# Dilated attention in a two-layer decoder: values in 512-byte pieces, attended tiles two and two, softmax steps behind the scores

## The chip, the cores and the metric

One core of one Trainium2 chip runs the whole program. The metric is the device time of one execution in microseconds, the median over several; a profiled execution also has a span, from the first to the last instruction on record, which is a little shorter. TensorE is PE below (PEld its weight loads), VectorE is DVE, ScalarE is ACT, GpSimd is POOL, SyncE is SP.

## What is computed

A trunk of two layers on a sequence of 1024 tokens of width 1024, all float32: a gated short convolution, a dilated attention, and a SwiGLU feed-forward block (width 2816) behind each. The change lies in the attention, cut here to what matters:

```python
BRANCHES = ((128, 1), (512, 4), (2048, 16))          # window, dilation; 16 heads of 64

def dilated_branch(q, k, v, rel_bias, window, dilation):
    ...                                              # regroup the tokens by residue mod dilation
    s = einsum(qb, kk) * HEAD_DIM ** -0.5            # a block of queries on its own and the previous keys
    s = s + bias                                     # T5 relative bias of the head
    s = where(mask, s, NEG_INF)
    lse = logsumexp(s)
    return einsum(exp(s - lse), vv), lse

def dilated_attention_mixer(h, w_qkv, w_out, rel_bias):
    ...
    alpha = softmax(stack(lses))                     # mixes the branches
    o = sum(alpha * outs)
    return o @ w_out
```

## The kernel before

Products of float32 quality are made of three passes with operands split into a high and a low part. `split` (L145, L146) does it: ACT copies `w_hi` (rounded), DVE subtracts to get `w_lo`. Both engines execute in the order in which the program was written; so does PE, and so do the queues that issue DMAs (SP's for loads).

The attention goes over 16 heads in slots, `slot(n, ...)` for n = 0 to 16. Slot n computes the scores of head n and, beside them, the softmax and the product with the values (PV) of head n - 1; in between stand pieces of other matrix work, drawn one by one from `dense` by `other(k)`: value tiles of later groups (`v` evictions on ACT), the projections of queries and keys, and the output product, whose weights and whose attended tiles (`oin`) are split on ACT and DVE as they come.

- Scores (`scores`): seven steps s0 to s6. PE fills a bank, DVE adds the bias on the way out: lf in s0 and s1 (two adds each, L1585), lh in s2 (L1594, with a first maximum, L1599), ld and lp together in s3 to s6 (L1611, L1616; two maxima in s4, L1620 and L1622). Behind s6 stand two more maxima, and POOL reduces m over the partitions to mb (L1628), the maximum by which the head is normalised.
- Softmax (`softmax`): five steps, for lf, lh, ld, and the two halves of lp (384 and 512 columns). Each subtracts mb on DVE (L1636) and takes the exponential on ACT (L1637). Slots 0 to 13 do the steps of the previous head one by one, between their own score steps. For heads 13 to 15 they all run at the end of the head's own slot.
- PV (`values`, L1647): PE multiplies exponentials with `vx`, in the order lf, lh, then ld and lp in turns. The tile `vx` holds the values of a pair of heads and between them columns of ones, so that one matmul gives the output o and the sum z. ACT copies z (logarithm, L1670) and o (L1671) out.
- A pair's o is scaled (`finish`, `attended`) and written to DRAM (`odram`), and read back as `oin` for the output product.
- SP loads, at the start of slot n, the keys, the values of the pair that is next (`load_values`, in even heads), the queries and the bias of head n + 1.

The start of each step in a slot up to 13:

```python
                for i in range(8):
                    next(due[0], None)      # a softmax step of head n - 1
                    next(sc, None)          # a score step of head n
                    k = 1 + (i in EXTRA and n < LAG) if n else i % 2
                    other(k)                # k pieces of the other matrix work
```

Of the kernel before, what the change touches and what calls it, by code (L numbers as in the profile page):

```python
# [10 lines left out]
F32 = mybir.dt.float32  # L11
F32R = mybir.dt.float32r
AF = mybir.ActivationFunctionType
# [7 lines left out]
H = 16  # L21
# [28 lines left out]
AO = 4  # L50
LAG = 13
EXTRA = (3, 7)
FILL = (("v", 0), ("v", 1), ("v", 2), ("v", 3), ("qk", 7))
DENSE = (13,) * 13 + (16, 13, 12, 11)
DEEP_ORDER = (1, 2, 5, 6, 7, 3, 4)

# [40 lines left out]
def view(t, off, dims):  # L97
    return bass.AP(tensor=t.tensor, offset=t.offset + off, ap=[t.ap[0]] + [list(d) for d in dims])
# [3 lines left out]
def trunk(ctx: ExitStack, tc: tile.TileContext, x, gains_in, cwi, ck, cwo, wqkv, wo, relb,  # L102
          wg, wu, wd, oneh, ident, out):
    nc = tc.nc
# [9 lines left out]
    scope = {}  # L114
# [20 lines left out]
    def split(src, dst=None, eng=nc.vector):  # L135

        w = src.shape[1]
        if dst is None:
            if w <= HALF:
                t = page("w", F32R)  # L140
                dst = t[:, :w], t[:, HALF:HALF + w]
            else:
                dst = page("w_hi", F32R)[:, :w], page("w_lo", F32R)[:, :w]
        hi, lo = dst
        nc.scalar.activation(hi, src, AF.Copy)  # L145
        eng.tensor_tensor(out=lo, in0=src, in1=hi, op=ALU.subtract)  # L146
        return hi, lo
# [200 lines left out]
    add_units(QK, QK_PAIRS, lambda u, n: wqkv[(KT, 0)[n] + u])  # L348
    for kind, g in FILL:
        if kind == "v":  # L350
# [1114 lines left out]
    def load_bias(h):  # L1465
        t = scope["pool"].tile([128, L1 + L2], F32, name="bias", tag="bias", bufs=2)
        base = tables.offset + h * G3
        nc.sync.dma_start(t[:, 0:L1], bass.AP(tensor=tables.tensor, offset=base, ap=[[1, 8], [A1, 16], [1, L1]]))
        nc.sync.dma_start(t[:, L1:L1 + L2], bass.AP(tensor=tables.tensor, offset=base + G0,
                                                    ap=[[1, 32], [A2, 4], [1, L2]]))  # L1470
        return t
# [8 lines left out]
    def attention(norm, qk):  # L1480
# [2 lines left out]
        qlo = [scope["pool"].tile([128, S], F32R, name=f"ql{a}") for a in range(2)]  # L1483
        for a in range(2):
            nc.gpsimd.memset(qlo[a][64 - 64 * a:128 - 64 * a].bitcast(F32), 0.0)
        vx = scope["pool"].tile([128, 16, 192], F32, name="vx", tag="vx", bufs=1)
        nc.vector.memset(vx[:, :, 64:128], 1.0)

        def projections(p):

# [37 lines left out]

        def load_values(p):
            src = vdram[p // 2]  # L1530
            for a in range(2):
                off = src.offset + p % 2 * 128 + a * 64
                dims = slice(128 * a, 128 * a + 64)
                nc.sync.dma_start(vx[:, 0:8, dims], bass.AP(src.tensor, off, [[256, 128], [128 * 256, 8], [1, 64]]))
                for h in range(2):
                    nc.sync.dma_start(vx[:, 8 + 4 * h:12 + 4 * h, dims],
                                        bass.AP(src.tensor, off + 512 * 256 * h, [[1024, 128], [256, 4], [1, 64]]))

        def load_kq(n):

# [99 lines left out]
        def values(p, a, st):  # L1640
            lf, lh, ld, lp = (st[n] for n in ("lf", "lh", "ld", "lp"))
            acc = [bank(), bank()]
            kd = [[128, 4], [1, 32]]
            b1 = [[32, 16], [1, 8]]

            def mm(ih, off, dims, u, rhs, first=False, last=False):
                nc.tensor.matmul(view(acc[ih], off, dims), vx[:, u, 64 * a:64 * a + 128], rhs,  # L1647
                                 start=first, stop=last)

            for ih in range(2):  # L1650
                for r4 in range(4):
                    mm(ih, r4 * 32, kd, 8 + r4, view(lf, ih * HALF + r4 * 32, kd), first=r4 == 0)
                    if r4 % 2:
                        yield
            for r4 in range(4):
                mm(1, r4 * 32, kd, 12 + r4, view(lh, r4 * 32, kd))
                if r4 % 2:
                    yield
            for j in range(8):
                off = (j % 4) * 8  # L1660
                mm(j // 4, off, b1, j, view(ld, blk(j), b1), last=False)
                if j:
                    mm(j // 4, off, b1, j - 1, view(lp, blk(j), b1), last=j % 4 == 3)
                yield
            o, z = st["o"], st["z"]
            n0 = slice(64 * a, 64 * a + 64)
            z0 = slice(64 - 64 * a, 128 - 64 * a)
            for ih in range(2):
                s = slice(ih * HALF, (ih + 1) * HALF)
                nc.scalar.activation(z[n0, s], acc[ih][z0], AF.Ln)  # L1670
                nc.scalar.activation(o[n0, s], acc[ih][n0], AF.Copy)  # L1671
            yield

        def finish(p):
# [39 lines left out]
        put_off, ending, due = [], [], [iter(())]  # L1714
        OZ, acts = {}, {}

        def slot(n, dense, ndense, late=0, hook=iter(())):

            def other(k):
                for _ in range(k):  # L1720
                    next(dense, None)

            p, a = divmod(n, 2)
            if n < H:
                new = dict(bias=bias.pop(n))
                sc = scores(p, a, new)
            else:
                sc = iter(())
            if n + 1 < H:
                load_kq(n + 1)  # L1730
                bias[n + 1] = load_bias(n + 1)
            if n:
                q, b = divmod(n - 1, 2)
                if b == 0:
                    OZ[q] = page("o"), page("z")
                old = live.pop(n - 1)
                old.update(o=OZ[q][0], z=OZ[q][1])
                pv = values(q, b, old)
            else:
                pv = iter(())  # L1740
            extra = later = iter(())
            lagged = n <= LAG
            if n + 1 < H:
                later = classes(n + 1)
            if lagged and a and p:
                ending.append(finish(p - 1))
            used = 0
            if lagged:
                for i in range(8):
                    next(due[0], None)  # L1750
                    next(sc, None)
                    k = 1 + (i in EXTRA and n < LAG) if n else i % 2
                    other(k)
                    used += k
                    if a and ending and i == 4:
                        run(ending.pop())
                run(sc)
            else:
                if a == 0 and not late:
                    other(1)  # L1760
                    used += 1
                for i in range(8):
                    next(sc, None)
                    next(pv, None)
                    next(pv, None)
                    if i >= late and i % 2 == 0:
                        other(1)
                        used += 1
                run(sc)
                run(pv)  # L1770
                if a == 0:
                    extra = finish(p - 1)
                if a == 0 and n < H:
                    load_values(p)
            left = max(ndense - used, 0)
            for i in range(8):
                next(pv, None)
                next(pv, None)
                if i == (2 if n > LAG + 1 else 5):
                    attended()  # L1780
                if not lagged and (i < FIN0 or i > SOFT):
                    next(extra, None)
                if i in (1, 2):
                    next(later, None)
                if i < 4:
                    next(hook, None)
                if i == (3 if lagged else SOFT) and n < H:
                    live[n] = new
                    due[0] = softmax(new)
                    if n >= LAG:  # L1790
                        run(due[0])
                other(left * (i + 1) // 8 - left * i // 8)
            run(pv)
            run(extra)

        def load_attended(ps):
            raw = {p: page("oin") for p in ps}
            for p in ps:
                nc.sync.dma_start(raw[p], odram[p])
            return raw  # L1800
# [27 lines left out]
        done, first = {}, {}  # L1828
# [7 lines left out]
                        yield from value_tiles(g, j)  # L1836
            yield from out_product(0, range(AO), first)

        def halves():
            for q, t in done.items():  # L1840
                first[q] = split(t)
                yield

        dense = fill()
        for n in range(H):
            if n == LAG - 2:
                done.update(load_attended(range(AO)))
            hook = halves() if n == LAG - 2 else iter(())
            slot(n, dense, DENSE[n], 3 if n == H - 2 else 0, hook)
            run(hook)  # L1850
        acts.update(split_attended(load_attended(range(AO, 7))))
        ensure(ahead_ao)
# [183 lines left out]
```

## Time and profile before

| what | value |
|---|---|
| median of 3 runs | 2103.48 us (2102.67 to 2103.56) |
| profiled execution | 2105.08 us, span 2103.3 us |
| granted PE clock, mean | 0.998 |
| busy: PE, PEld, DVE, ACT, POOL | 99%, 85%, 83%, 48%, 11% of the span |
| DMA moved | 300.70 MB, mean 143 GB/s; 48236 of 141495 packets under 512 B |

A row of a group reads: line, engine, operation, out<-in with the names of the program, shape, count, then busy time, mean of one, and the idle time before it with what ended it. A row of a timeline begins with start and duration in microseconds. SPq is SP's issuing of DMAs. The attention lies at about 1110 to 1430 us of the span.

### The profile page before, as it was taken

The numbers are of one execution on the slowest core, as the hardware profiler recorded it, in microseconds if no ns is written. First come the engines' busy times: TensorE is split into PE (matmuls) and PEld (weight loads), VectorE is DVE, ScalarE is ACT, GpSimd is POOL, SyncE is SP. The second block draws the span as 40 slices with busy tenths as digits, with TensorE's granted clock in tenths as the row PEclk, the third lists the DMA queues.
The fourth block names the chain that finished last, engine by engine and source line by source line (L and its number), as shares of the span: only waits on it lengthen the run. The fifth ranks groups of instructions, "written<-read, shape, count | busy, mean of one in ns | idle before, by whom it ended". The sixth has DMA issues, their size and how long they took to land. (4 is left out here: it accounts for less than half of the span.)

```text
span 2103.3 us, 30766 instructions
## 1 busy us (share of the span) xinstructions
PE 2083.1 (99%) x10990; PEld 1792.2 (85%) x10990; DVE 1746.1 (83%) x3264; ACT 1013.7 (48%) x1852; POOL 240.0 (11%) x336
## 2 busy tenths in 40 slices
PE   9999999999999999999999999999999999999998
PEld 7788888888888888887789999988788888888887
DVE  8898769988888788968984778987998888888886
ACT  7433427444444454445553566555544434456433
POOL 1000000110101010010223232211011001001000
PEclk9999999999999999999999999999999999999999
DMA  7322643233333467452658788955223323368432
GB/s 216 100 96 71 230 135 76 101 105 111 102 105 110 145 201 208 133 159 65 232 201 209 161 202 210 250 165 154 71 87 108 107 99 113 110 194 245 158 96 80
DMA packets 141495, 300.70 MB, mean 143 GB/s; under 512 B 48236, under 2 KB 54462, under 8 KB 141344
## 3 DMA queue, kind: packets, MB, share of 16 engines
q1 hardware_dynamic: 107488, 201.94, 32.4%
q0 software_dynamic: 26224, 82.11, 12.6%
q10 hardware_dynamic: 7632, 14.70, 1.9%
q8 instruction: 87, 1.43, 0.3%
q14 instruction: 64, 0.52, 0.1%
HBM read 208.42 MB, written 82.93 MB: 139 GB/s over the span
## 5 line engine op out<-in xcount | busy, mean ns | idle before, releaser
L573 PE MATMUL bank<-b,w 128*128 128x512 f32 x1980 | 772.5, 390 | 5.4 <-DVE w L146 5.2
L571 PE MATMUL bank<-b,w 128*128 128x512 f32 x1980 | 772.3, 390 | 2.3 <-ACT w L145 1.1
L572 PE MATMUL bank<-b,w 128*128 128x512 f32 x1980 | 771.9, 390 | 0.6 <-DVE b L882 0.6
L573 PEld LDWEIGHTS bank<-b,w 128*128 128x128 f32 x1980 | 372.0, 188 | 87.5 <-DVE w L146 10.5
L571 PEld LDWEIGHTS bank<-b,w 128*128 128x128 f32 x1980 | 372.3, 188 | 80.3 <-ACT w L145 1.9
L572 PEld LDWEIGHTS bank<-b,w 128*128 128x128 f32 x1980 | 372.3, 188 | 76.6 <-DVE b L882 1.2
L145 ACT ACTIVATE w<-combo 128x512 fp32r<-128x512 f32 (+2 forms) x492 | 251.5, 541 | 238.9 <-DVE combo L193 219.7
L146 DVE TENSOR_TENSOR w<-combo,w 128x512 fp32r<-128x512 f32 (+2 forms) x492 | 279.8, 582 | 37.8 <-ACT w L145 37.0
L577 ACT ACTIVATE part<-bank 128x512 f32<-128x512 f32 x189 | 112.5, 595 | 383.9 <-PE bank L573 378.7
L146 DVE TENSOR_TENSOR w<-raw,w 128x512 fp32r<-128x512 f32 (+2 forms) x345 | 194.4, 585 | 36.5 <-ACT w L145 36.5
L581 DVE TENSOR_TENSOR part<-part,bank 128x256 f32<-128x256 f32 (+1 forms) x369 | 173.1, 499 | 31.9 <-PE bank L573 17.3
L145 ACT ACTIVATE w<-raw 128x512 fp32r<-128x512 f32 (+2 forms) x345 | 168.5, 531 | 47.8 <-PE bank L573 12.2
L373 PE MATMUL bank<-w_hi,w 128*128 128x512 f32 (+1 forms) x400 | 151.0, 378 | 0.1
L375 PE MATMUL bank<-w_hi,w 128*128 128x512 f32 (+1 forms) x400 | 149.3, 373 | 0.7 <-DVE w L146 0.7
L374 PE MATMUL bank<-w_lo,w 128*128 128x512 f32 (+1 forms) x400 | 149.0, 373 | 0.0
L801 DVE TENSOR_TENSOR x<-x,bank 128x512 f32<-128x512 f32 x136 | 92.9, 683 | 28.7 <-PE bank L573 28.7
L492 DVE TENSOR_TENSOR x<-x,bank 128x512 f32<-128x512 f32 (+1 forms) x104 | 66.7, 644 | 59.8 <-PE bank L375 58.9
L193 DVE TENSOR_TENSOR combo<-raw 128x512 f32<-128x512 f32 (+1 forms) x174 | 112.6, 648 | 0.0
L375 PEld LDWEIGHTS bank<-w_hi,w 128*128 128x128 f32 x400 | 75.3, 188 | 14.8 <-DVE w L146 1.6
L564 DVE TENSOR_TENSOR b<-hin,b 128x512 fp32r<-128x512 f32 x126 | 79.5, 686 | 9.4 <-ACT b L563 9.4
L373 PEld LDWEIGHTS bank<-w_hi,w 128*128 128x128 f32 x400 | 75.5, 189 | 12.3 <-ACT w L145 0.5
L374 PEld LDWEIGHTS bank<-w_lo,w 128*128 128x128 f32 x400 | 75.5, 189 | 11.9
(234 smaller groups left out, 3377.0 us busy)
## 6 DMA issues: line engine op xcount, KB each, us to landing
hin<-part SPq DMA_DIRECT2D x126, 256.0 KB
raw<-in_ffn_w_gate SPq DMA_DIRECT2D x44, 512.0 KB
raw<-in_ffn_w_up SPq DMA_DIRECT2D x44, 512.0 KB
part<-sum POOLq DMA_DIRECT2D x72, 256.0 KB, 2.3
raw<-in_ffn_w_down SPq DMA_DIRECT2D x48, 384.0 KB
raw<-in_attn_w_qkv SPq DMA_DIRECT2D x27, 512.0 KB
raw<-in_conv_w_in SPq DMA_DIRECT2D x24, 512.0 KB
part<-part POOLq DMA_DIRECT2D x36, 256.0 KB, 2.6
```

The lines of the kernel that those rows point to most:

```text
L145: nc.scalar.activation(hi, src, AF.Copy)
L146: eng.tensor_tensor(out=lo, in0=src, in1=hi, op=ALU.subtract)
L193: eng.tensor_tensor(out=c, in0=a, in1=b, op=op)
L373: nc.tensor.matmul(b, whi[:, a], ahi[:, s], start=first, stop=False)
L374: nc.tensor.matmul(b, whi[:, a], alo[:, s], start=False, stop=False)
L375: nc.tensor.matmul(b, wlo[:, a], ahi[:, s], start=False, stop=last)
L571: nc.tensor.matmul(b, hi[:, a], bhi, start=start and k == 0, stop=False, skip_group_check=True)
L572: nc.tensor.matmul(b, hi[:, a], blo, start=False, stop=False, skip_group_check=True)
L573: nc.tensor.matmul(b, lo[:, a], bhi, start=False, stop=k == n - 1, skip_group_check=True)
L577: nc.scalar.activation(t, b, AF.Copy)
L581: nc.vector.tensor_tensor(out=t, in0=t, in1=b, op=ALU.add)
L801: nc.vector.tensor_tensor(out=X[n][:, half(h)], in0=X[n][:, half(h)], in1=b, op=ALU.add)
```

## The change

Three things are changed together.

1. `vx` becomes [ones 64 | head a=0 64 | head a=1 64], repeated 16 times, and 64 ones behind. The two heads' values lie next to each other, so one DMA brings both: three DMAs a pair in place of six, each piece 512 bytes in place of 256. The left operand of PV is [ones, v0] for one head and [v1, ones] for the other, z and o lie in the other halves of the accumulator.
2. The attended tiles 0 to 3, loaded and split in slot 11, are now loaded and split two in slot 10 (0 and 1) and two in slot 11 (2 and 3), and their loads are issued behind the keys and the bias of the next head.
3. In slots up to 13 the score step comes first, and the softmax step is left out in the first round, so that each softmax step stands two score steps later against the scores.

```diff
+OIN = LAG - 2
...
-        vx = scope["pool"].tile([128, 16, 192], F32, name="vx", tag="vx", bufs=1)
-        nc.vector.memset(vx[:, :, 64:128], 1.0)
+        vx = scope["pool"].tile([128, 16 * 192 + 64], F32, name="vx", tag="vx", bufs=1)
+        nc.vector.memset(view(vx, 0, [[192, 17], [1, 64]]), 1.0)
...
         def load_values(p):
             src = vdram[p // 2]
-            for a in range(2):
-                off = src.offset + p % 2 * 128 + a * 64
-                dims = slice(128 * a, 128 * a + 64)
-                nc.sync.dma_start(vx[:, 0:8, dims], bass.AP(src.tensor, off, [[256, 128], [128 * 256, 8], [1, 64]]))
-                for h in range(2):
-                    nc.sync.dma_start(vx[:, 8 + 4 * h:12 + 4 * h, dims],
-                                        bass.AP(src.tensor, off + 512 * 256 * h, [[1024, 128], [256, 4], [1, 64]]))
+            off = src.offset + p % 2 * 128
+            nc.sync.dma_start(view(vx, 64, [[192, 8], [1, 128]]),
+                              bass.AP(src.tensor, off, [[256, 128], [128 * 256, 8], [1, 128]]))
+            for h in range(2):
+                nc.sync.dma_start(view(vx, (8 + 4 * h) * 192 + 64, [[192, 4], [1, 128]]),
+                                  bass.AP(src.tensor, off + 512 * 256 * h, [[1024, 128], [256, 4], [1, 128]]))
...
-                nc.tensor.matmul(view(acc[ih], off, dims), vx[:, u, 64 * a:64 * a + 128], rhs,
+                nc.tensor.matmul(view(acc[ih], off, dims), vx[:, u * 192 + 128 * a:u * 192 + 128 * a + 128], rhs,
...
-            z0 = slice(64 - 64 * a, 128 - 64 * a)
+            o0 = slice(64 - 64 * a, 128 - 64 * a)
...
-                nc.scalar.activation(z[n0, s], acc[ih][z0], AF.Ln)
-                nc.scalar.activation(o[n0, s], acc[ih][n0], AF.Copy)
+                nc.scalar.activation(z[n0, s], acc[ih][n0], AF.Ln)
+                nc.scalar.activation(o[n0, s], acc[ih][o0], AF.Copy)
...
             if n + 1 < H:
                 load_kq(n + 1)
                 bias[n + 1] = load_bias(n + 1)
+            done.update(load_attended(ps))
...
                 for i in range(8):
-                    next(due[0], None)
                     next(sc, None)
+                    if i > 0:
+                        next(due[0], None)
...
-        def halves():
-            for q, t in done.items():
-                first[q] = split(t)
+        def halves(ps):
+            for q in ps:
+                first[q] = split(done.pop(q))
                 yield
...
-            if n == LAG - 2:
-                done.update(load_attended(range(AO)))
-            hook = halves() if n == LAG - 2 else iter(())
-            slot(n, dense, DENSE[n], 3 if n == H - 2 else 0, hook)
+            ps = {OIN - 1: (0, 1), OIN: (2, 3)}.get(n, ())
+            hook = halves(ps)
+            slot(n, dense, DENSE[n], 3 if n == H - 2 else 0, hook, ps)
```

PE's instructions keep their order. Below, line numbers after the change are one higher than before in the helpers (L146 becomes L147), and the same in the scores and the softmax.

DVE in slot 2 (scores of head 2, softmax of head 1), before: from the ld subtraction to that of lp's second half.

```order
L1636 TENSOR_TENSOR ld<-ld,mb 128x1024
L1594 TENSOR_TENSOR lh<-bank,bias 128x512
L1599 TENSOR_TENSOR m<-lf,lh 128x512
L1636 TENSOR_TENSOR lp<-lp,mb 128x16x24
L1611 TENSOR_TENSOR ld<-bank,bias 128x16x16
L1616 TENSOR_TENSOR lp<-bank,bias 128x16x16
L146 TENSOR_TENSOR w_lo<-raw,w_hi 128x1024
L1636 TENSOR_TENSOR lp<-lp,mb 128x512
```

The same stretch after the change, from s3's adds on (ahead of it stand all four lf adds, lh's add and maximum):

```order
L1611 TENSOR_TENSOR ld<-bank,bias 128x16x16
L1616 TENSOR_TENSOR lp<-bank,bias 128x16x16
L1636 TENSOR_TENSOR ld<-ld,mb 128x1024
L147 TENSOR_TENSOR w_lo<-raw,w_hi 128x1024
L1611 TENSOR_TENSOR ld<-bank,bias 128x16x16
L1616 TENSOR_TENSOR lp<-bank,bias 128x16x2x8
L1620 TENSOR_TENSOR m<-lf,ld 128x512
L1622 TENSOR_TENSOR m<-m,lp 128x16x24
L1636 TENSOR_TENSOR lp<-lp,mb 128x16x24
L1611 TENSOR_TENSOR ld<-bank,bias 128x16x16
L1616 TENSOR_TENSOR lp<-bank,bias 128x16x16
L1636 TENSOR_TENSOR lp<-lp,mb 128x512
```

The first lp subtraction has moved behind the weight split's w_lo and behind the four instructions of s4; the second stands behind s5.

ACT in the same slot, before:

```order
L145 ACTIVATE w_hi<-raw 128x1024
L1637 ACTIVATE lf<-lf 128x1024
L1637 ACTIVATE lh<-lh 128x512
L1637 ACTIVATE ld<-ld 128x1024
L1637 ACTIVATE lp<-lp 128x16x24
L1522 ACTIVATE v<-bank,scales 128x256
L145 ACTIVATE w_hi<-raw 128x1024
L1637 ACTIVATE lp<-lp 128x512
```

and after:

```order
L146 ACTIVATE w_hi<-raw 128x1024
L1637 ACTIVATE lf<-lf 128x1024
L1637 ACTIVATE lh<-lh 128x512
L1637 ACTIVATE ld<-ld 128x1024
L1523 ACTIVATE v<-bank,scales 128x256
L146 ACTIVATE w_hi<-raw 128x1024
L1637 ACTIVATE lp<-lp 128x16x24
L1637 ACTIVATE lp<-lp 128x512
```

The exponential of lp's first half has moved behind v's eviction and the second w_hi.

SP from the end of slot 10's loads to slot 11's (odram_85 to 88 are the attended tiles 0 to 3), before:

```order
L159 DMA raw<-in_attn_w_out 128x512 x2
L1799 DMA oin<-odram_85 128x1024
L1799 DMA oin<-odram_86 128x1024
L1799 DMA oin<-odram_87 128x1024
L1799 DMA oin<-odram_88 128x1024
L1546 DMA ka<-kq_1_2926 64x1024
L1547 DMA ka<-kq_1_2926 64x1024
L1534 DMA vx<-vdram_95 128x8x64
L1536 DMA vx<-vdram_95 128x4x64 x2
L1534 DMA vx<-vdram_95 128x8x64
L1536 DMA vx<-vdram_95 128x4x64 x2
L1551 DMA qa<-kq_0_2925 64x1024 x2
```

and after:

```order
L1801 DMA oin<-odram_85 128x1024
L1801 DMA oin<-odram_86 128x1024
L160 DMA raw<-in_attn_w_out 128x512 x2
L1546 DMA ka<-kq_1_2926 64x1024
L1547 DMA ka<-kq_1_2926 64x1024
L1533 DMA vx<-vdram_95 128x8x128
L1536 DMA vx<-vdram_95 128x4x128 x2
L1551 DMA qa<-kq_0_2925 64x1024 x2
L1552 DMA ql_10192<-kq_0_2925 64x1024
L1469 DMA bias<-tables 128x1x361
L1470 DMA bias<-tables 128x1x349
L1801 DMA oin<-odram_87 128x1024
```

Tiles 0 and 1 now go ahead of the two weight pieces, tiles 2 and 3 behind head 12's keys, the values of pair 5, the queries and the bias; vx takes three issues, of twice the width. (Tile 3, odram_88, is the next row.)

More of the change, by code (lines that the diff above doesn't have):

```diff
@@ L1715, in attention, with slot @@
         OZ, acts = {}, {}
-        def slot(n, dense, ndense, late=0, hook=iter(())):
+        def slot(n, dense, ndense, late=0, hook=iter(()), ps=()):
             def other(k):
```

## The prediction

> **What bounds the kernel now.** I read the page first, then the busy time by stage over the attention, the waits of PE there and behind it, and last the rows of single slots. The page's first lines, busy time per engine:
>
> ```profile
> span 2103.3 us, 30766 instructions
> PE 2083.1 (99%) x10990; PEld 1792.2 (85%) x10990; DVE 1746.1 (83%) x3264; ACT 1013.7 (48%) x1852; POOL 240.0 (11%) x336
> ```
>
> PE is busy for all but 20 us of the span. The attention, where every edit of the change lies, runs from about 1110 to 1430 us. Its busy time in windows (columns: PE, PEld, DVE, ACT, POOL, granted clock, DMA share, GB/s), one window and the sum over 1100 to 1420:
>
> ```profile
> 1300.00:1340.00 40.00, 40.00 (x275) 36.70 (x274) 37.67 (x60) 24.81 (x34) 11.32 (x9) 1.00 1.07 288
> sum 320.00, PE 319.21 PEld 305.73 DVE 247.50 ACT 179.75 POOL 85.41; mean PE 39.90 PEld 38.22 DVE 30.94 ACT 22.47 POOL 10.68
> ```
>
> PE stands still for 0.8 us of these 320. The waits of PE (us in total, times, longest), first those inside the attention, then those from 1420 us to the end:
>
> ```profile
> PE bank L1574 <- ACT o L1671: 0.8, 1, 0.8
> ...
> PE bank L573 <- DVE w L146: 1.5, 2, 1.1
> PE bank L663 <- DVE part L581: 0.5, 1, 0.5
> PE bank L571 <- ACT part L577: 0.4, 1, 0.4
> ```
>
> Two things follow. There is under 1 us here for the change to win. And whatever makes PE wait inside the attention moves the end by the same amount, since behind it only 2.4 us of waits could swallow any of it. So the question is which of PE's inputs the change makes late. PE's own order does not change at all.
>
> **The subtractions behind the scores.** This edit decides. In each slot DVE subtracts the previous head's maximum (lf, lh, ld, and lp in two halves), ACT takes the exponential, and PE multiplies with vx (PV): lf first, lp last. Now each subtraction stands two score steps later. What that is meant to fill is the wait of DVE for the reduced maximum, ahead of the lf subtraction:
>
> ```profile
>   POOL mb L1628: 32.9, 13
> ```
>
> DVE has that time to spare, but PE never waits for it. What counts is how early lp is ready. An ordinary slot (3): the end of the first lp exponential, and PE's first use of it:
>
> ```profile
> 1178.91 0.53 ACT L1637 ACTIVATE lp<-lp 128x384 f32<-128x384 f32 x1 [0.74 <-DVE lp L1636]
> 1182.52 0.28 PE L1647 MATMUL bank<-lp,vx 128*128 128x128 f32 x1
> ```
>
> It is ready 3.1 us early. The move puts the adds and maxima of two steps ahead of it, at most 2.6 us by the rows below, so such a slot keeps a margin and costs nothing. Slots with a weight split inside the softmax are different: ACT makes w_hi, DVE waits for it to make w_lo, and both queues are in order. Slot 2, DVE:
>
> ```profile
> 1155.16 1.22 DVE L1636 TENSOR_TENSOR lf<-lf,mb 128x1024 f32<-128x1024 f32 x1
> 1156.29 0.75 DVE L1585 TENSOR_TENSOR lf<-bank,bias 128x256 f32<-128x256 f32 x2
> 1156.96 0.68 DVE L1636 TENSOR_TENSOR lh<-lh,mb 128x512 f32<-128x512 f32 x1
> ...
> 1158.22 1.22 DVE L1636 TENSOR_TENSOR ld<-ld,mb 128x1024 f32<-128x1024 f32 x1
> 1159.36 0.68 DVE L1594 TENSOR_TENSOR lh<-bank,bias 128x512 f32<-128x512 f32 x1
> 1160.07 0.69 DVE L1599 TENSOR_TENSOR m<-lf,lh 128x512 f32<-128x512 f32 x1
> 1160.68 0.55 DVE L1636 TENSOR_TENSOR lp<-lp,mb 128x384 f32<-128x384 f32 x1
> ...
> 1163.13 1.23 DVE L146 TENSOR_TENSOR w_lo<-raw,w_hi 128x1024 fp32r<-128x1024 f32 x1 [1.23 <-ACT w_hi L145]
> 1164.27 0.68 DVE L1636 TENSOR_TENSOR lp<-lp,mb 128x512 f32<-128x512 f32 x1
> ...
> 1165.54 0.68 DVE L1620 TENSOR_TENSOR m<-lf,ld 128x512 f32<-128x512 f32 x1
> 1166.26 0.56 DVE L1622 TENSOR_TENSOR m<-m,lp 128x384 f32<-128x384 f32 x1
> ```
>
> ACT, and then PE's first use of the two halves of lp:
>
> ```profile
> 1159.47 1.06 ACT L1637 ACTIVATE ld<-ld 128x1024 f32<-128x1024 f32 x1 [1.17 <-DVE ld L1636]
> ...
> 1161.70 0.46 ACT L1522 ACTIVATE v<-bank,scales 128x256 f32<-128x256 f32 x1
> 1162.05 1.05 ACT L145 ACTIVATE w_hi<-raw 128x1024 fp32r<-128x1024 f32 x1
> 1164.99 0.63 ACT L1637 ACTIVATE lp<-lp 128x512 f32<-128x512 f32 x1 [1.89 <-DVE lp L1636]
> ```
>
> ```profile
> 1165.60 0.39 PE L1647 MATMUL bank<-lp,vx 128*128 128x128 f32 x2
> 1166.94 0.39 PE L1647 MATMUL bank<-lp,vx 128*128 128x128 f32 x2
> ```
>
> An instruction starts some 0.08 us before the one ahead ends, so a step is the distance of two starts: lf subtraction 1.13, lh 0.60, ld 1.14, a pair of 256-wide adds 0.67, lh add 0.71, its maximum 0.61, w_lo 1.14, the two maxima of the fourth diagonal step's group 0.72 and 0.47. (The first ld and lp adds have the size of the lf adds.) In the new order, from 1155.16: four lf adds 1.34, lf subtraction 1.13, lh add and maximum 1.32, lh subtraction 0.60, ld and lp add 0.67, ld subtraction 1.14: DVE is through with ld at 1161.4. ACT takes the ld exponential to 1162.5, then v (0.35 by starts) and w_hi, which now stand **ahead** of the lp exponential, to 1163.8. DVE waits for w_hi, makes w_lo to 1165.0, the next step's adds and maxima (0.67 + 0.72 + 0.47) to 1166.85, the lp subtraction to 1167.40; the exponential ends at 1167.95. PE wants it at 1165.60: it waits **2.4 us** (1.8 to 2.8, half a us either way). The second half follows by adds, subtraction and exponential (0.67, 0.68, 0.63) at 1169.3, when PE, now 2.4 late, wants it at 1169.3: nothing more.
>
> Slot 5 holds two splits:
>
> ```profile
> 1205.19 0.48 ACT L1522 ACTIVATE v<-bank,scales 128x256 f32<-128x256 f32 x1
> 1205.07 0.75 DVE L1585 TENSOR_TENSOR lf<-bank,bias 128x256 f32<-128x256 f32 x2
> 1218.36 0.39 PE L1647 MATMUL bank<-lp,vx 128*128 128x128 f32 x2
> ```
>
> Now w_hi comes straight behind v, ends at 1206.6, w_lo is out of DVE's way by 1207.75. Then lf adds 0.67, lf subtraction 1.13, lh add and maximum 1.32, lh subtraction 0.60, adds 0.67, ld subtraction 1.14, adds and maxima 1.86, lp subtraction: 1215.7, exponential 1216.2. Only then the second w_hi, behind it on ACT, to 1217.2; w_lo to 1218.4, adds 0.67, lp's second subtraction to 1219.7, exponential 1220.3. PE wants this half at 1218.36: **1.9 us** (1.2 to 2.3).
>
> Slot 8 has a split between lf and lh:
>
> ```profile
> 1256.56 0.76 DVE L1585 TENSOR_TENSOR lf<-bank,bias 128x256 f32<-128x256 f32 x2
> 1268.46 0.39 PE L1647 MATMUL bank<-lp,vx 128*128 128x128 f32 x2
> ```
>
> Four adds and the lf subtraction to 1259.1, lf exponential to 1260.2, w_hi to 1261.2, w_lo to 1262.3, then 1.32, 0.60, 0.67, 1.14, 1.86 and 0.55 to 1268.5, exponential 1269.0: **0.6 us** (0 to 1).
>
> Slot 14 already waits, for the copies of o that stand on ACT behind head 13's exponentials; these follow the reduction and the five subtractions without a gap:
>
> ```profile
> 1362.44 1.23 DVE L1636 TENSOR_TENSOR lf<-lf,mb 128x1024 f32<-128x1024 f32 x1 [2.82 <-POOL mb L1628]
> 1369.09 0.33 PE L1574 MATMUL bank<-qa,kca 128*128 128x128 f32 x1 [0.76 <-ACT o L1671]
> ```
>
> So the wait grows or shrinks with the end of slot 13's maxima. Slot 13 has weight splits and accumulations among its steps; its subtractions end later against the scores, and I put the end of its maxima 0.8 us later, an estimate of about one subtraction (0.55 to 0.68): **+0.8** (from -0.8, the wait gone, to +2.6, the two steps in full).
>
> **The values in pieces of 512 bytes and the other edits.** Half the packets, three issues on SP in place of six, the same bytes. No row of PE waits names vx, so a shorter transfer moves nothing: 0. The pair is now loaded whole, when its last reader is done; the second half had to wait for that already. Ones and values have traded places: z is read from the accumulator's own partitions and o across, one activation of the same size each, 0. The attended tiles: two are split in slot 10, two in slot 11. A pair is 2.3 us of DVE time by w_lo's step; in slot 10 it stands behind the last maxima, where DVE waits for the reduction anyway, and slot 11 is rid of it: 0. Tiles 0 and 1 are issued ahead of two pieces of attn_w_out, which go out two issues later, weights that are split a slot or more after: 0. The other two loads are the doubt. Tiles 2 and 3 are issued behind head 12's bias, not ahead of its keys. The SP rows of the second half of vx and of the last bias, ACT's first use of an attended tile and the kca copy behind it, and PE's first score of slot 12:
>
> ```profile
> 1307.82 1.63 SPq L1534 DMA_DIRECT2D vx<-vdram  x1
> 1315.95 0.55 SPq L1469 DMA_DIRECT2D bias<-tables  x1
> 1317.34 1.04 ACT L145 ACTIVATE w_hi<-oin 128x1024 fp32r<-128x1024 f32 x1
> 1318.29 1.13 ACT L1558 ACTIVATE kca<-ka 128x512 fp32r<-128x512 f32 x1
> 1325.64 0.37 PE L1574 MATMUL bank<-qa,kca 128*128 128x256 f32 x1
> ```
>
> The last bias issue ends at 1316.5; with three vx issues less ahead of it (0.55 to 1.63 each, the issues above) the tiles go out between 1313 and 1316.5. At the 288 GB/s of that window 0.5 MB takes 1.8 us, so ACT has tile 2 by 1318.5 or so. Behind it stand w_hi (1.04) and the kca copy (1.13) that slot 12 needs at 1325.64: five us of margin, 0. The Trainium skill, "DMA: Bandwidth & Descriptors", Specifications, gives 512 B as the least transfer at line rate. By this rule the vx load ahead of the tiles is shorter and the margin larger; no run here shows it yet.
>
> **The rivals.** *Covered*: the slots' later exponentials are absorbed, so that the end does not move measurably. The place is the same, the price 0 to 4.2 us: if only slot 2 waits in full and the 2.4 us of waits behind the attention swallow it, nothing is left (2103.5); if 5, 8 and 14 take their lower ends (1.2 + 0 - 0.8), 2.2 to 2.8 us are left, 2106. It decides at the point where ACT's w_hi in slot 2 no longer stands behind the ld exponential; the order on both queues speaks against that. *Faster*: the 0.8 us of slot 14 vanish and no slot is late, 2102.7. That is less than a measurement can tell, and over 0.2% would need 4.2 us of PE time that stands idle nowhere here. *Loads late*: tile 2 lands after 1323.5, or vx after its PV start, and kca or PE waits for it; each us late costs one, some 3 us on top of the forecast, 2112. The DMA share of 1.07 speaks for it, the margin of five us against it. *Clock*: PE's longest wait in the quoted rows is 1.1 us, with a granted clock of 1.00 in the window quoted; slot 2's wait would be twice that, and if the clock fell behind it, PE would run the next microseconds slower, one to three us more, 2111. The Trainium skill, "TensorE: Matmul & The Clock Gate", HAM oscillation, puts the limit at idle gaps of about 3.4 us; by that rule a wait of 2.4 us leaves the clock alone, and no run here shows a gap of that size.
>
> **How the numbers follow.** 2.4 + 1.9 + 0.6 + 0.8 = 5.7 us on the profiled execution, whose time is 2105.08 (its span 2103.3 and 1.8 around it): 2110.8. That execution lies 1.6 above the median of the runs, 2103.48; on the median it is **2109.2 us**, 0.27% slower. The bounds of the terms add up to 2.2 (1.8 + 1.2 + 0 - 0.8) and 8.7: 2105.7 to 2112.2. About 0.2%, 4.2 us, is what a measurement of this kernel can tell from no change, so slower begins at 2107.7. Chances: the stalls as counted 0.68, of which 0.08 below 4.2 us; covered 0.18; loads late 0.05; clock 0.04; faster 0.05, of which 0.03 by over 0.2% for something that the trace hides. Slower 0.60 + 0.05 + 0.04 = 0.69; same 0.08 + 0.18 + 0.02 = 0.28; faster 0.03. The range takes in the forecast's bounds and part of covered and of the late loads: 2104.5 to 2112.8.
>
> **What would show it.** In the new profile: PE waits at L1647 for ACT's lp in slots 2, 5 and 8, with 2 us or more in slot 2, and DVE's wait for mb down by a third or more. PE rows without such waits prove the forecast wrong; so does a wait for vx or for an attended tile in its place. A time below 2105 would mean that the order of ACT's queue does not hold lp back as worked out here.

## The result, and the profile after

The changed kernel takes 2113.24 us (median of 4 runs, 2111.54 to 2114.96) against 2103.40 before (4 runs, 2102.67 to 2103.56): 9.8 us or 0.47% slower, ratio 1.0047 with a 95% interval of 1.003 to 1.0065. The forecast was 2109.2 us, with a range up to 2112.8. The direction and the place were right, the size was not.

The page after, and under it the waits of PE inside the attention (us in total, times, longest):

```profile
span 2113.2 us, 30740 instructions
PE 2088.7 (99%) x10990; PEld 1797.5 (85%) x10990; DVE 1746.4 (83%) x3264; ACT 1013.1 (48%) x1852; POOL 239.1 (11%) x336
```

```profile
PE bank L1647 <- ACT lp L1637: 4.8, 3, 2.4
PE bank L1574 <- ACT o L1671: 0.8, 1, 0.8
PE bank L1647 <- DVE x L493: 0.5, 1, 0.5
```

These are 6.1 us of waits where there were 0.8. But PE is also *busy* 5.6 us longer (2088.7 against 2083.1) with the same 10990 matmuls: something made them slower. The timeline of PE in slot 2 shows where:

```profile
1163.59 0.61 PE L1647 MATMUL bank<-ld,vx 128*128 128x128 f32 x4
1166.59 0.80 PE L1647 MATMUL bank<-lp,vx 128*128 128x128 f32 x2 [2.40 <-ACT lp L1637]
1167.18 0.63 PE L1647 MATMUL bank<-ld,vx 128*128 128x128 f32 x2
...
1171.02 0.39 PE L1647 MATMUL bank<-ld,vx 128*128 128x128 f32 x2
```

Two matmuls that take 0.39 us at 1171.0 took 0.63 us right behind the wait. Windows cut at the instants at which the granted clock changes (columns: PE, PEld, DVE, ACT, POOL, clock, DMA share, GB/s), for the waits in slots 2, 5 and 14:

```profile
1163.14:1166.55 3.41, 1.06 (x10) 0.86 (x8) 3.38 (x8) 0.52 (x1) 0.00 (x0) 1.00 0.38 109
1166.55:1169.97 3.42, 3.38 (x16) 3.38 (x17) 2.52 (x6) 2.69 (x4) 0.68 (x1) 0.50 0.19 44
...
1221.17:1224.58 3.41, 1.47 (x13) 1.43 (x13) 3.38 (x9) 2.11 (x4) 0.08 (x1) 1.00 0.10 38
1224.58:1227.99 3.41, 3.41 (x18) 3.41 (x18) 0.85 (x1) 3.22 (x5) 3.41 (x1) 0.50 0.46 135
...
1374.77:1378.18 3.41, 2.14 (x17) 1.78 (x16) 2.50 (x4) 3.36 (x8) 0.00 (x0) 1.00 0.04 12
1378.18:1381.59 3.41, 3.41 (x18) 3.41 (x18) 3.38 (x8) 0.36 (x1) 0.55 (x1) 0.50 0.38 154
```

Each wait falls into a window of 3.41 us in which PE was busy 1.06, 1.47 and 2.14 us, and in the next 3.41 us the clock stands at 0.50 and PE gets half as far: 1.7 us lost each time, 5.1 us for the three. The waits themselves came as worked out. In slot 2 the weight split stands ahead of lp on both engines:

```profile
1160.98 0.47 ACT L1523 ACTIVATE v<-bank,scales 128x256 f32<-128x256 f32 x1
1161.35 1.05 ACT L146 ACTIVATE w_hi<-raw 128x1024 fp32r<-128x1024 f32 x1
1166.02 0.52 ACT L1637 ACTIVATE lp<-lp 128x384 f32<-128x384 f32 x1 [3.62 <-DVE lp L1636]
```

```profile
1162.43 1.23 DVE L147 TENSOR_TENSOR w_lo<-raw,w_hi 128x1024 fp32r<-128x1024 f32 x1 [2.57 <-ACT w_hi L146]
...
1165.43 0.55 DVE L1636 TENSOR_TENSOR lp<-lp,mb 128x384 f32<-128x384 f32 x1
```

DVE stands 2.57 us for w_hi with lp's subtraction queued behind, and PE waits 2.40. In slot 5 the second w_hi ends on ACT at 1219.9, its w_lo on DVE at 1221.2, and lp's second exponential at 1223.1. PE in slots 5, 8 and 14:

```profile
1223.15 0.49 PE L1647 MATMUL bank<-lp,vx 128*128 128x128 f32 x2 [1.94 <-ACT lp L1637]
...
1275.53 0.49 PE L1647 MATMUL bank<-lp,vx 128*128 128x128 f32 x2 [0.45 <-ACT lp L1637]
...
1375.41 1.16 PE L1647 MATMUL bank<-lf,vx 128*128 128x128 f32 x8 [0.47 <-DVE x L493]
...
1377.37 0.33 PE L1574 MATMUL bank<-qa,kca 128*128 128x128 f32 x1 [0.80 <-ACT o L1671]
```

The wait of DVE that the late subtractions were to fill, for the reduced maximum ahead of lf, is 8.5 us where it was 32.9. But DVE now stands elsewhere. The lf adds come first, and DVE waits for PE's scores instead (DVE's idle time ahead of instructions on lf, after):

```profile
  PE bank L1575: 25.8, 11
  POOL mb L1628: 8.5, 4
```

The same line before:

```profile
  PE bank L1575: 4.5, 2
```

Most of the idle time has moved and has not gone.

### The profile page after: what moved, and what is told of

It is laid out like the page before. It is cut to its first block, busy times and chain, and to the rows that moved or that the text cites. A ratio compares the mean times of both kernels' runs of the same rounds, so it can differ in the third digit from the quotient of the medians.

```text
span 2113.2 us, 30740 instructions
## 1 busy us (share of the span) xinstructions
PE 2088.7 (99%) x10990; PEld 1797.5 (85%) x10990; DVE 1746.4 (83%) x3264; ACT 1013.1 (48%) x1852; POOL 239.1 (11%) x336
## 5 line engine op out<-in xcount | busy, mean ns | idle before, releaser
L146 ACT ACTIVATE w<-combo 128x512 fp32r<-128x512 f32 (+2 forms) x492 | 251.5, 541 | 237.7 <-DVE combo L194 212.2
L147 DVE TENSOR_TENSOR w<-combo,w 128x512 fp32r<-128x512 f32 (+2 forms) x492 | 279.7, 582 | 37.8 <-ACT w L146 37.0
L147 DVE TENSOR_TENSOR w<-raw,w 128x512 fp32r<-128x512 f32 (+2 forms) x345 | 194.3, 585 | 37.1 <-ACT w L146 37.1
L146 ACT ACTIVATE w<-raw 128x512 fp32r<-128x512 f32 (+2 forms) x345 | 168.6, 531 | 45.7 <-PE bank L574 11.5
```

## The experiments

The theory: all of the loss is the softmax order; it makes PE wait, and a wait that leaves PE idle for most of a 3.41 us window also halves its clock for the next one. The first rival: the loads (values, attended tiles) bring part of it. The second: the clock has no part in it. The third: the clock falls by the length of the wait alone.

**The two load changes without the order.** Edit, on the changed kernel:

```diff
                 for i in range(8):
-                    next(sc, None)
-                    if i > 0:
-                        next(due[0], None)
+                    next(due[0], None)
+                    next(sc, None)
```

> The change without its third part: values in pieces of 512 bytes and attended tiles two and two, softmax steps in their old places. Theory (all of the loss is the order of the softmax): 2103.4 us, within 0.5 us of before, no wait of PE for lp, the 0.8 us wait for o in slot 14 still there or gone. Rival (the loads cost too: late tiles, or transfers that collide): 2105 or more, with a PE wait behind a DMA or behind kca.

2104.33 us (11 runs, 2102.11 to 2107.01), ratio 1.0004 (0.9995 to 1.0013): no difference that can be told, so the bulk of the loss is not here. But the trace has a wait that before has not; ACT's first attended tile in slot 11, and PE's waits in the attention:

```profile
1321.61 1.06 ACT L146 ACTIVATE w_hi<-oin 128x1024 fp32r<-128x1024 f32 x1 [5.32 <-DMA oin<-odram]
```

```profile
PE bank L1574 <- ACT o L1671: 0.7, 1, 0.7
PE bank L1647 <- DVE lp L1616: 0.7, 1, 0.7
```

Tile 2 comes 5.3 us late for ACT, DVE's split of it ends late, and PE waits 0.7 us in slot 12 for a bank that DVE empties behind it.

**The order alone.** The same edit the other way round, on the kernel before.

> The third part alone: the old loads, softmax steps behind the scores. Theory: 2111 to 2115 us as with the whole change, PE waits for lp of 2.4 us in slot 2 and 1.9 us in slot 5, and the granted clock at 0.5 for 3.4 us behind both. Rival (the loads bring a part of the loss): 2109 us, the sum of the waits alone.

2113.44 us (4 runs), ratio 1.0048 (1.0034 to 1.0061): the whole loss. Its waits for lp:

```profile
PE bank L1647 <- ACT lp L1637: 5.4, 4, 2.3
```

They are 2.25, 2.06, 0.52 and 0.57 us; the clock is at 0.50 behind the first two. In slot 14 PE waits as in the whole change, and its window holds the same 2.14 us of work, but the clock stays at 1.00 behind it.

**PE kept busy where it waited.** The whole change with matmuls of zeros in the way:

```diff
+FILLER = {(1, 1): 21, (4, 4): 17}      # the second kernel: 11 and 9
...
             for j in range(8):
                 off = (j % 4) * 8
                 mm(j // 4, off, b1, j, view(ld, blk(j), b1), last=False)
+                for _ in range(FILLER.get((2 * p + a, j), 0)):
+                    mm(j // 4, 0, kd, 8, view(zcol, 0, [[0, 4], [0, 32]]))
                 if j:
```

> The whole change, with 21 matmuls of zeros ahead of lp's first half in slot 2 and 17 ahead of its second half in slot 5 (0.11 us each, added to the accumulator, the sums stay as they are): PE is busy where it waited 2.4 and 1.9 us, and gets its exponentials no earlier. Theory (the surplus over the waits is the clock, which falls for 3.4 us behind a stretch in which PE was busy too little): 3.3 to 3.6 us less than the whole change, 2109.5 to 2110, clock 1.00 behind slots 2 and 5. Rival (the surplus has another cause): the time of the whole change, 2113, or more.

> The same with 11 and 9 matmuls of zeros: PE still waits 1.2 us in slot 2 and 1.0 us in slot 5. Theory: a wait of that size leaves PE busy for over 60 percent of any 3.4 us, so the clock stays up and the time is that of the full filling, 2109.5 to 2110. Rival (any wait of a microsecond brings the clock down): 2113.

I had the size of a matmul wrong: in float32 each is two passes, 0.22 us, as the 42 records of the first kernel in slot 2 show, and the 22 of the second:

```profile
1164.40 4.85 PE L1648 MATMUL bank<-zcol,vx 128*128 128x128 f32 x42
```

```profile
1164.27 2.62 PE L1648 MATMUL bank<-zcol,vx 128*128 128x128 f32 x22
```

So the second kernel is the one that fills the waits exactly, and the first fills them twice over. The first comes out as its rival said (2113 or more), but it is no test of what was meant. The second takes 2110.24 us (5 runs), 3.0 less than the whole change (2113.24), although no exponential comes earlier and PE does useless work all the time that it had waited. The windows around the filled waits of slots 2 and 5:

```profile
1163.00:1167.00 4.00, 4.00 (x36) 3.87 (x35) 3.96 (x9) 0.52 (x1) 0.00 (x0) 1.00 0.37 113
1167.00:1171.00 4.00, 4.00 (x36) 4.00 (x37) 2.30 (x5) 3.46 (x5) 1.47 (x1) 1.00 0.09 18
...
1221.00:1225.00 4.00, 3.96 (x34) 3.77 (x34) 3.17 (x6) 3.73 (x6) 1.73 (x1) 1.00 0.08 9
```

The clock stays at 1.00. That is the expected saving of two windows, 3.4 us, within the spread of these runs. The two profiles say it more sharply. Going by the starts of matching matmuls against the profile of before, from 1100 to 1430 us, PE falls 11.5 us behind in the whole change and 6.5 with the waits filled: 5.0 less, which is three windows. The third is slot 14's: the waits there are the same in both (0.5 and 0.8 us), and with the others filled the clock behind them happens to stay at 1.00. The first kernel, 2114.35 us, pays 4.1 us for 18 more matmuls (4.0 us by 0.22 each), which is PE time at face value. So the surplus over the waits was the clock.

**Waits of chosen size.** The kernel before with lp's first half copied onto itself on ACT, so that its exponential is late in six slots:

```diff
                 nc.scalar.activation(dst, dst, AF.Exp)
+                if dst is lp1:
+                    for _ in range(DOSE.get(n, 0)):
+                        nc.scalar.activation(dst, dst, AF.Copy)
                 yield
```

> The kernel before, with the first exponential of lp held back on ACT in six slots by 9, 14, 14, 19, 20 and 16 copies of lp's first half onto itself (0.45 to 0.5 us each; heads 2, 3, 5, 6, 8, 11), so that PE waits of some 0.9, 1.5, 2.1, 2.7, 3.0 and 2.2 us arise, the estimate being copies less the time by which lp was early before. Theory (the clock is set window by window of 3.41 us by how long PE was busy in the one before, the limit lying at about 0.6): the 0.9 us leaves the clock at 1.00, waits of 2.7 us and more halve it for one window, those between by where the grid of windows cuts them. Rival (only a window that is idle as a whole, 3.4 us, halves it): no drop at all.

> As the first kernel with held-back exponentials, with 10, 17, 11, 18, 16 and 10 copies, for PE waits of 2 to 3 us, the sizes of the change's. Theory (the busy share of PE in a window of a fixed grid decides, the limit between 0.46 and 0.63): each wait that leaves some window under 0.46 is followed by one window at half clock, each that leaves all windows over 0.63 by none; waits of one size can fall on either side by where the grid cuts them. Rival (the length of the wait alone decides): one length parts drops from none.

The sizes came out other than meant (0.58 us where 1.5 was, 5.52 where 2.2 was), and the single times, 2130.76 and 2128.39 us, say nothing by themselves. The traces do. The clock changes only on a grid of 3.41 us. The table has the waits of the two kernels of this section, with windows cut on that grid and PE's busy time as a share of the window:

| head | wait of PE, us | PE busy in the windows that it touches | clock in the window behind |
|---|---|---|---|
| 3, first kernel | 0.58 | 0.83 | 1.00 |
| 2, first | 1.78 | 0.57 | 1.00 |
| 11, second | 2.18 | 0.36 | 0.50 |
| 5, second | 2.19 | 0.36 | 0.50 |
| 3, second | 2.25 | 0.47 | 1.00 |
| 2, second | 2.35 | 0.31 | 0.50 |
| 6, second | 2.91 | 0.46, then 0.69 | 1.00, 1.00 |
| 6, first | 3.46 | 0.58, then 0.41 | 1.00, 0.50 |
| 5, first | 3.91 | 0.03 | 0.50 |
| 8, second | 4.31 | 0.65, then 0.08 | 1.00, 0.50 |
| 8, first | 4.98 | 0.41, then 0.13 | 0.50, 0.50 |
| 11, first | 5.52 | 0.20, then 0.19 | 0.50, 0.50 |

Two pairs of rows make the point, from the second kernel, the wait of 2.35 us and that of 2.25 us:

```profile
1182.64:1186.05 3.41, 1.06 (x10) 0.87 (x9) 2.04 (x5) 3.28 (x8) 1.16 (x1) 1.00 0.62 154
1186.05:1189.47 3.42, 3.42 (x19) 3.42 (x18) 2.36 (x2) 3.40 (x5) 2.64 (x2) 0.50 1.01 231
...
1203.12:1206.53 3.41, 1.59 (x14) 1.39 (x13) 0.49 (x1) 3.22 (x7) 2.89 (x1) 1.00 0.45 72
1206.53:1209.95 3.42, 2.99 (x26) 3.00 (x27) 0.73 (x1) 3.40 (x6) 1.87 (x4) 1.00 0.20 38
```

A wait of 2.25 us whose window still holds 1.59 us of work costs no clock, one of 2.18 us in a window with less does, and one of 2.91 us cut by the grid into two does not. So the length of the wait alone does not decide. Nor does it take a window that is idle as a whole: windows with PE busy for 0.41 of them were followed by half clock too. In all traces of this case every window with a share of 0.45 or less was followed by half clock. Between 0.46 and 0.63 it went both ways: slot 14's window, 2.14 of 3.41 us, fell in the whole change and did not in the order alone, and 0.57 and 0.58 above did not. What tells these apart stays open, and the ends of matmuls in the records are modelled. Above 0.64 none fell.

**One step later instead of two.** On the changed kernel, the softmax step also in the first round:

```diff
                     next(sc, None)
-                    if i > 0:
-                        next(due[0], None)
+                    next(due[0], None)
```

> The whole change with the score step first, but the softmax step in the first round too, so that each subtraction stands one score step later than before, not two. Theory (what counts is the weight split and the adds between ld and the last lp): by the rows of before, lp's first half is out ahead of w_hi in all slots; in slot 2 its second half comes behind w_lo and the fourth diagonal step's group, exponential at 1168.1 against 1166.94, a PE wait of 1.2 us, too short for the clock: 1.2 to 1.6 us above the kernel with the loads alone (2104.3), 2105.5 to 2106. Rival (every step later costs alike, half of two steps): half of the loss, 2108 to 2109.

2107.2 us (10 runs, 2106.58 to 2109.16), ratio 1.0019 (1.0009 to 1.0028), between the two ranges expected. PE's waits:

```profile
PE bank L1647 <- ACT lp L1637: 1.2, 1, 1.2
PE bank L1647 <- DVE lp L1616: 1.0, 1, 1.0
PE bank L1574 <- ACT o L1671: 0.8, 1, 0.8
PE bank L1647 <- DVE x L493: 0.5, 1, 0.5
```

The 1.2 us in slot 2 is as worked out, the only wait for lp, and the clock stays at 1.00 behind it. The time lies 2.9 us above the loads alone, where 1.2 to 1.6 were expected. The 0.5 us in slot 14 is what I left out. The 1.0 us in slot 12 explains little of it, since the loads alone have such a wait too (0.7). About half a microsecond of the miss stays open, within the spread of these runs.

**The old order in four slots.**

```diff
+EARLY = (2, 5, 8, 13)
...
+                    if n in EARLY:
+                        next(due[0], None)
                     next(sc, None)
-                    if i > 0:
+                    if i > 0 and n not in EARLY:
                         next(due[0], None)
```

> The whole change, with the softmax steps in their old places in slots 2, 5, 8 and 13 alone. Theory: all waits of PE for lp are gone, and with them the clock's; the time is that of the loads alone, 2104.3, and not below before, since PE had nothing to win: 2103.4 to 2104.6. Rival (the other late slots cost something that the waits don't show): 2106 or more.

2104.8 us (11 runs, 2102.89 to 2108.24), ratio 1.0006 (0.9997 to 1.0015): with the steps put back in four of the slots the loss is gone to within what can be told, though in the other slots they still stand two steps late. What is left in the trace of the attention, beside slot 14's wait of before, is the tiles, ACT and then PE:

```profile
1325.20 1.06 ACT L147 ACTIVATE w_hi<-oin 128x1024 fp32r<-128x1024 f32 x1 [3.56 <-DMA oin<-odram]
```

```profile
1327.33 0.39 PE L1575 MATMUL bank<-qa,kca 128*128 128x256 f32 x1 [1.37 <-ACT kca L1559]
```

The kca copy stands behind the late tile, and PE waits 1.37 us at the start of slot 12.

**The values alone, and the tiles ahead.** The first has only the 512-byte pieces. The second is the kernel with both load changes, with this edit:

```diff
+            done.update(load_attended(ps))
             if n + 1 < H:
                 load_kq(n + 1)
                 bias[n + 1] = load_bias(n + 1)
-            done.update(load_attended(ps))
```

> The values in pieces of 512 bytes alone, attended tiles and softmax as before. Theory: no PE wait changes, 2103.4, within 0.5 us of before; the 0.9 us by which the kernel with both load changes lay above (unclear) is that of the attended tiles 2 and 3, which came 5.3 us late for ACT there. Rival (the whole load of a pair collides): 2104.3.

> The loads alone once more (softmax in its old places), with the attended tiles 0 and 1, and 2 and 3, issued ahead of the keys, values and bias of the slot and not behind them; they are split two and two as in the change. Theory (the late issue made tiles 2 and 3 land at 1321.6 to 1325 us, and kca or the scores' adds behind their split came late for PE by 0.7 to 1.6 us): no wait of ACT for these tiles over 1 us, no PE wait in slots 11 and 12, the time of before, 2103.5, against 2104.3 and 2104.8 with the late issue. Rival (the split two and two costs by itself): 2104.3.

2103.70 us (11 runs; ratio 1.0003, 0.9994 to 1.0012) and 2103.39 us (11 runs; 1.0000, 0.9991 to 1.0009): both are the kernel before. With the tiles issued ahead, ACT takes tile 2 without a wait at

```profile
1318.72 1.04 ACT L146 ACTIVATE w_hi<-oin 128x1024 fp32r<-128x1024 f32 x1
```

and the view of PE's waits has none in the attention, not even the one of slot 14. The time is still that of before: under a microsecond was all there was to win, as the windows of before said. None of these kernels beats it by an amount that can be told.

## Why the prediction was wrong in size

- *What bounds the kernel*: right. PE without any wait in the attention (tiles ahead) runs in the same time.
- *Slot 2*: 2.4 us forecast, 2.40 measured, by the chain named (w_hi, w_lo, adds, lp). *Slot 5*: 1.9 and 1.94. *Slot 8*: 0.6 and 0.45. *Slot 14*: +0.8 forecast, and 0.47 + 0.80 - 0.76 = 0.51 measured, in two waits; by the starts of its matmuls PE loses 0.8 there. The maxima of slot 13 end 8.3 us later than before where PE is 7.5 late, so they are 0.8 later against PE, as put. That size was an estimate of one subtraction and nothing in the rows forced it, so its closeness is partly luck. The new wait of 0.47 is not the one foreseen: PE waits for a bank that DVE's addition to x empties, and that addition stands behind the late subtractions. Together 5.7 forecast, 5.3 measured.
- *The step that failed*: that a wait costs its own length and matmuls go on at full clock behind it. The case "clock" had a chance of 0.04. Its first ground was thin: the longest wait quoted, 1.1 us, lies at 1495 us, and the clock of 1.00 quoted with it belongs to the window 1300 to 1340 (behind that wait it was 1.00 as well). Its second was the Trainium skill, which gives an idle gap of about 3.4 us as the limit ("TensorE: Matmul & The Clock Gate", HAM oscillation). The runs differ from that, and the measurement decides: waits of 2.40 and 1.94 us, and 0.47 + 0.80 close together, were each followed by 3.41 us at half clock. What counts in these traces is how much PE was busy in a window, except for the middle shares that stay open, and where the grid puts the window. The profile of before had a sign of it that was not read: its half-clock window at 9.0 to 12.4 us stands behind one in which PE was busy for 2.02 of 3.41 us, without a single gap over 0.6 us. The price was also put on slot 2 alone, "one to three us"; three windows came, 5.1 us.
- *The sum as it is*: 5.3 of waits, some 0.2 more at each of the four places (the record's idle begins at a modelled end; back to back, the next matmul would have started 0.17 earlier), 0.3 in slot 12, 5.1 of clock: 11.4 us in the attention. Matmul by matmul against the profile of before, PE is 11.5 us later behind the attention than ahead of it. Both profiles hold one half-clock window in the first 65 us, but the waits there differ (the longest gap is 1.94 us before, 1.56 after), and by 65 us PE is 1.6 us earlier after the change than before, which leaves the 9.9 us between the spans. Where the grid lies is new in each run, which fits the spread of 2111.5 to 2115.0 after.
- *The attended tiles, "five us of margin, 0"*: wrong by itself, hidden in the whole change. I gave 0.5 MB 1.8 us at the window's mean rate and had tile 2 at 1318.5. Issued by 1312.1 in the kernel with both loads, it was there at 1321.6, or 1323.7 on the clock of the profile of before, where PE is 2.1 us later. In those 9.5 us 2.6 MB moved (276 GB/s), which is about the tile and the 2.1 MB of values, queries and bias issued ahead of it: the wrong step was that the tile would move alone. The case "loads late" named the right chain (kca behind the tile) for the kernel with the old order in four slots, 1.4 us of PE waits; with the loads alone it is DVE's adds behind the tile's split, 0.7. No median with its interval could tell either, and in the whole change PE is 7 us late there and loses 0.3 us.
- *The values*: 0 forecast, 0 measured (ratio 1.0003). *DVE's wait for mb*: down by three quarters, and worth nothing, as forecast; most of it went over to waits for PE's scores.

## What to carry to other kernels

When PE is the bound, as here, filling the idle time of another engine earns nothing, and whatever that moves behind a step on an in-order queue has to be traced to the next product that waits for it: here a weight split between two softmax steps. A PE wait of two microseconds can cost nearly four: the wait, and half of the 3.41 us window behind it, unless the grid happens to leave enough work in each window. So read PE's busy time window by window and add up short waits that lie close together. If such a wait can't be avoided, matrix work in it, here only useless matmuls, can keep the clock up.

## What was new about the hardware

- In all twelve traces the granted clock changes only on a grid of 3.41 us, whose place differs from run to run; a window in which PE was busy for 0.45 or less was always followed by one at 0.50, one above 0.64 never.
- 20 useless matmuls, 4.4 us of PE time, put into two waits made the program 3.0 us faster (2110.24 against 2113.24).
- A 0.5 MB tile issued behind some 2 MB of other loads took 9.5 us from issue to use, at 276 GB/s in that stretch.
